# All projections in pairs of chunks, and attention's twelve steps in eight visits, in a two-layer encoder on one core

## The chip, the core and the metric

The kernel runs on one core of a Trainium2 chip. The core has five engines that run side by side, each through its own queue in order: TensorE (PE: matmuls and transposes, results in PSUM), VectorE (DVE), ScalarE (ACT), GpSimd (POOL), and SyncE (SP), which here issues nearly all DMA transfers. PE's loads of its stationary operand are listed apart, as PEld. PSUM has eight banks; this program uses four for projections and four for everything else. The metric is device time in microseconds of one execution; a kernel's time is the median of its runs.

## The reference

Two layers over 256 tokens of width 1024 in float32, each with a token mixer and a gated feed-forward part with a width-3 convolution. The change lies in the token mixer:

```python
u, q, k, v, g_pool, g_attn = jnp.split(xn @ w_in, SPLITS, axis=-1)
...
pooled = jnp.stack([_centred_mean(ug[:, :, gi], w) for gi, w in enumerate(POOL_WINDOWS)], axis=2) - ug
pool_out = jnp.einsum('bsgc,gcd->bsgd', pooled, w_pool).reshape(B, S, POOL_WIDTH) * pool_scale
...
outs.append(o_g)
lses.append(lse_g)
wts = jax.nn.softmax(jnp.stack(lses, axis=0), axis=0)
attn = jnp.einsum('gbsh,gbshd->bshd', wts, jnp.stack(outs, axis=0).astype(jnp.float32))
...
merged = jax.nn.sigmoid(g_pool) * (pool_out @ w_a) + jax.nn.sigmoid(g_attn) * (attn_out @ w_b)
return merged @ w_o
```

There are 12 heads of width 128 in three groups with dilations 1, 4 and 16. Head hh of each of the three groups is combined into output head hh, so four output heads remain.

## The kernel before, in words

**Precision by parts.** Every operand is split in two reduced-precision parts, high and low, and a product is the sum of high x high, low x high and high x low. The class `Weights` (line 95) loads 1 MB blocks of weights into three raw buffers by SP (L131) and splits each into pieces of 128 x 1024: ScalarE casts the high part `wh` (L191), VectorE subtracts for the low part `wl` (L192). Five pieces of each part are in SBUF at most (`BUFS`), and `get` splits up to three pieces past the one that it hands out. `free` gives a piece's buffers back.

**A chunk.** `proj` (L539) makes one chunk of 128 output columns for all 256 tokens. The moving operand holds the high and low parts of the activations side by side, so a chunk is eight wide matmuls (`wh`, 512 columns) and eight narrow ones (`wl`, 256 columns) into one PSUM bank, 16 in all. `proj(x2, n)` makes n chunks at one call of `two_sums` (L506), keeps the results in the list `ready`, and hands out one at a time; a later call takes what is ready and issues nothing. `two_sums` does all wide matmuls of its chunks and then all narrow ones, or the other way round, and turns the order round at each call, so that one call ends with the kind that the next begins with. The banks of a chunk are emptied by ScalarE and VectorE, by `add_up` (L567 and L568) for u, the gates and po2, and by L1055 to L1067 for q and k. Four banks (`mmp`) rotate among the projections, the pool sums and some smaller uses; four others (`acc`) serve values, attention and the output products.

**The order of a layer's token mixer.** Values; then u, eight chunks (L889 to L899), with the pooling windows on VectorE after every second; then q and k in six rounds m of four chunks (L1039), in the order `PAIRS`. In round m == 1 each of the four chunks comes after one of four pool parts (`pool_out`, L929), two calls of `two_sums` with two k-steps each, whose sums go through ScalarE (L943), VectorE (L944), ScalarE (L947) and VectorE (L948). From m == 3 on, one step of attention is issued after every second chunk. Then eight chunks over the pool outputs `po2` (L1074), with the other six steps between them; then eight chunks of gates, and so on.

**Attention's steps.** `scores(hh)` (L961): 14 matmuls into two banks, then VectorE (L976 adds the bias table `bt`, L981 takes the maximum), ScalarE (L984, the exponential) and VectorE (L986, L987). `turn(hh)` (L992): eight transposes of the probabilities (L999) into two banks, three copies by ScalarE and three operations of VectorE. `weigh(hh)` (L1010): 14 matmuls with the values, then one operation each of ScalarE and VectorE. Twelve steps are taken from a list, head a and head b of a pair interleaved:

```python
steps += [(scores, a), (turn, a), (scores, b), (weigh, a), (turn, b), (weigh, b)]
...
if m >= 3 and n % 2:
    step()
...
if c not in (1, 6):
    step()
```

Before, u was in single chunks in layer 0 and in pairs in layer 1 (`1 + (l > 0)`), q and k were in pairs but for m == 1, the chunks over po2 were single, and the gates were in pairs.

**What sets the order on an engine.** The framework orders instructions at build time by their place in the program and by when its timing model has their inputs ready; TensorE's order in the trace is that of the program in the changed stretch, while VectorE and ScalarE mix splits, emptying and attention as they come ready. `issue_after` ties a block behind a given instruction; it holds the bias table's transfers (L394 to L398), which are issued ahead of the first projection of pool group 1 in layer 0, behind the last weight load on SP.

Of the kernel before, what the change touches and what calls it, by code (L numbers as in the profile page):

```python
# [18 lines left out]
S = 256  # L19
# [12 lines left out]
PAD = 8  # L32
# [188 lines left out]
def encoder(ctx, tc, x, w_in, w_pool, pool_scale, w_a, w_b, w_o, norm1, norm2, w_up, conv_w,  # L221
# [13 lines left out]
    def cols(w, c0):  # L235

        src = w[:, c0 : c0 + 256].rearrange("(k p) c -> p k c", p=P)
        return W.add(
            src, (8, 256), [((lambda t, j=j: t[:, :, j * P : (j + 1) * P]), (8, P)) for j in (0, 1)]
        )  # L240
# [10 lines left out]
    for l in range(DEPTH):  # L251
# [24 lines left out]
        for c in range(2):  # L276
            W.use(cols(w_in[l], C_GA + c * 512))
            W.use(cols(w_in[l], C_GA + c * 512 + 256))
            src = w_b[l][:, c * 512 : (c + 1) * 512].rearrange("(k p) c -> p k c", p=P)
# [11 lines left out]
        for f in range(0, NF, 2):  # L291
            a = cols(w_up[l], f * P) if f >= ENTRY else []
# [213 lines left out]
    def two_sums(x2, nk, *chunks):  # L506

        wide, rests = ([(c, k, kind) for c in chunks for k in range(nk)] for kind in (True, False))
        first = rests if turns["rest"] else wide
        last = wide if turns["rest"] else rests
        for steps in (first, last):
            for (ps, wh, wl), k, kind in steps:
                out, w, x = (ps, wh, x2[:, k]) if kind else (ps[:, 1], wl, x2[:, k, 0])
                nc.tensor.matmul(  # L519
                    out, w(k), x, start=(steps is first and k == 0),  # L520
                    stop=(steps is last and k == nk - 1), skip_group_check=turns["rest"],
                )
        turns["rest"] = not turns["rest"]
# [15 lines left out]
    def proj(x2, n=1):  # L539


        if not ready:
            pieces = [W.get() for _ in range(n)]
            ps = [mmp.tile([P, 2, S], F32, tag="mm", name="proj_ps") for _ in range(n)]
            two_sums(
                x2, KD,
                *(
                    (b, lambda k, wh=wh: wh[:, k, :], lambda k, wl=wl: wl[:, k, :])
                    for b, (_, (wh, wl)) in zip(ps, pieces)
                ),  # L550
            )
            for i, _ in pieces:
                W.free(i)
            ready.extend((b[:, 0], b[:, 1]) for b in ps)
        return ready.pop(0)

    def halves(a):

        return a.rearrange("p (t m) -> p t m", t=2)

    def in_order(a):

        return a.rearrange("p (m t) -> p t m", t=2)

    def add_up(out, sums):

        nc.scalar.copy(out=out, in_=sums[1])  # L567
        nc.vector.tensor_add(out=out, in0=sums[0], in1=out)  # L568
# [90 lines left out]
    def two_parts(tag, name):  # L659


        return big.tile([P, KD, 2, 2, P], F32R, tag=tag, name=name)
# [174 lines left out]
    for l in range(DEPTH):  # L837
# [21 lines left out]
        if l == 0:  # L859
            with tc.manual_schedule():  # L860
                begun = begin_values_of_x()
            x2 = first_values(*begun, keep_values)
# [26 lines left out]
        for gi in range(3, -1, -1):  # L889
            w = WINDOWS[gi]  # L890
            u = sm.tile([P, 2, S + 2 * PAD], F32, tag="u", name="u")
            nc.vector.memset(u[:, :, 0:PAD], 0.0)
            nc.vector.memset(u[:, :, PAD + S :], 0.0)
            for j in range(2):
                if l == 0 and (gi, j) == (1, 0):

                    with tc.issue_after(W.last.ins):
                        next(bias)
                add_up(in_order(u[:, j, PAD : PAD + S]), [halves(a) for a in proj(x2, 1 + (l > 0))])  # L899
            cur, n = u, S + 2 * PAD  # L900
            sh = 1
            while sh < w:
                nxt = sm.tile([P, 2, S + 2 * PAD], F32, tag="us", name="us")
                n -= sh
                nc.vector.tensor_add(
                    out=nxt[:, :, 0:n], in0=cur[:, :, 0:n], in1=cur[:, :, sh : sh + n]
                )
                cur = nxt
                sh *= 2
            hw = w // 2  # L910
            o = PAD - hw
            e = edge[:, gi, 0:hw].unsqueeze(1).to_broadcast([P, 2, hw])
            nc.vector.tensor_mul(out=cur[:, :, o : o + hw], in0=cur[:, :, o : o + hw], in1=e)
            if hw > 1:
                e = edge[:, gi, hw : w - 1].unsqueeze(1).to_broadcast([P, 2, hw - 1])
                r = slice(o + S - hw + 1, o + S)
                nc.vector.tensor_mul(out=cur[:, :, r], in0=cur[:, :, r], in1=e)
            pd = sm.tile([P, 2, S], F32, tag="us", name="pd")
            nc.vector.scalar_tensor_tensor(
                out=pd, in0=cur[:, :, o : o + S], scalar=1.0 / w, in1=u[:, :, PAD : PAD + S],  # L920
                op0=ALU.mult, op1=ALU.subtract,
            )
            both = pl2[gi // 2][:, gi % 2 * 2 : gi % 2 * 2 + 2]
            ph, pl = both[:, :, 0], both[:, :, 1]
            pd = pd.rearrange("p k (m t) -> p k t m", t=2)
            nc.scalar.copy(out=ph, in_=pd)
            nc.vector.tensor_sub(out=pl, in0=pd, in1=ph.bitcast(F32))
            pooled[gi] = both
# [96 lines left out]
            nc.scalar.copy(out=oh, in_=ps)  # L1025
            nc.vector.tensor_sub(out=ol, in0=ps, in1=oh.bitcast(F32))

        steps = []
        for pair in ((0, 1), (2, 3)):
            a, b = pair  # L1030
            steps += [(scores, a), (turn, a), (scores, b), (weigh, a), (turn, b), (weigh, b)]

        def step():
            if steps:
                f, hh = steps.pop(0)
                f(hh)


        for m, c in enumerate(PAIRS):  # L1039
            if m == 1:  # L1040
                po2 = two_parts("m2", "po2")
                pool_parts = pool_out(po2)
            if m == 2:

                qkl = big.tile([P, 2, HPG, 2, P], F32R, tag="xn", name="qkl")
                ql, kl = qkl[:, 0], qkl[:, 1]
            for n in range(4):
                if m == 1:
                    next(pool_parts)
                src, rest = (halves(a) for a in proj(x2, 1 + (m != 1)))  # L1050
                hd = 2 * c + n % 2
                scale = HD**-0.5 if n < 2 else 1.0
                if hd < HPG:
                    hi, lo = ((qh, ql) if n < 2 else (kh, kl))
                    nc.scalar.mul(out=hi[:, hd], in_=src, mul=scale)  # L1055
                    nc.vector.scalar_tensor_tensor(
                        out=lo[:, hd], in0=src, scalar=scale, in1=hi[:, hd].bitcast(F32),
                        op0=ALU.mult, op1=ALU.subtract,
                    )
                    nc.vector.scalar_tensor_tensor(  # L1060
                        out=lo[:, hd], in0=rest, scalar=scale, in1=lo[:, hd].bitcast(F32),
                        op0=ALU.mult, op1=ALU.add,
                    )
                else:
                    o = (q if n < 2 else kk)[:, hd - HPG]
                    nc.scalar.mul(out=o, in_=rest, mul=scale)
                    nc.vector.scalar_tensor_tensor(  # L1067
                        out=o, in0=src, scalar=scale, in1=o, op0=ALU.mult, op1=ALU.add
                    )
                if m >= 3 and n % 2:  # L1070
                    step()

        pa = big.tile([P, KD, S], F32, tag="ybig", name="pa")
        for c in range(KD):  # L1074
            add_up(pa[:, c, :], proj(po2))
            if c not in (1, 6):
                step()
        assert not steps


        gates = big.tile([P, 4, S], F32, tag="gates", name="gates")
# [14 lines left out]
        for c4 in range(2):  # L1096
            ths = [gate(4 * c4 + j) for j in range(4)]
            for j2 in range(2):
# [3 lines left out]
                for j, ps in enumerate(both):  # L1102
                    c = 4 * c4 + 2 * j2 + j
                    m = sm.tile([P, S], F32, tag="u", name="m")
# [5 lines left out]
                    m = halves(m)  # L1110
# [4 lines left out]
        x2 = two_parts("x", "x2")  # L1115
# [114 lines left out]
        if l + 1 < DEPTH:  # L1230
            x2 = two_parts("x", "x2")
# [34 lines left out]
```

## Time and profile before

| | us |
|---|---|
| median of 3 runs | 875.19 |
| runs | 874.42 to 875.40 |
| the profiled execution | 874.7 |
| its span, first to last instruction | 872.8 |
| TensorE busy | 865.6 (99%) |
| VectorE busy | 680.1 (78%) |
| ScalarE busy | 526.1 (60%) |
| mean granted TensorE clock | 0.998 |

The page gives each engine's busy share in 40 slices of the span (digits are tenths), the chain of work that ended last, and groups of instructions with busy time, mean duration and the idle time before them. A row of the chain in order of time has a start, a length and what ran, with the number of matmuls behind x; its lengths run from one piece's modelled end to the next one's. A row of a timeline has start, length, engine, line, operation and operands. In both, L followed by a number is a line of the kernel.

### The profile page before, as it was taken

How to read it: one execution, taken by the hardware profiler on the slowest of the kernel's cores; microseconds unless marked ns; L12 is line 12 of the kernel's file. 1: busy time of each engine (PE TensorE's matmuls, PEld its weight loads, DVE VectorE, ACT ScalarE, POOL GpSimd, SP SyncE). 2: the span in 40 equal slices, each digit the busy share in tenths (PEclk: the TensorE clock that was granted, in tenths of full speed). 3: DMA queues.
4: the chain of work that ended last, by engine and by line, in shares of the span. 5: the costliest groups of instructions: out<-in, count | busy, mean ns of one | idle time of the engine just before them, and what ended most of it. 6: DMA issues, size and time to landing. Idle time of an engine off the chain costs nothing.

```text
span 872.8 us, 12725 instructions
## 1 busy us (share of the span) xinstructions
PE 865.6 (99%) x4807; PEld 756.8 (87%) x4807; DVE 680.1 (78%) x1158; ACT 526.1 (60%) x927; POOL 31.3 (4%) x98
## 2 busy tenths in 40 slices
PE   9999999999999999999999999999999999999997
PEld 8888889988888888888888889999888888888886
DVE  7998786757869978878855987776678698887874
ACT  7656554556647766666545674545666486666662
POOL 1800000000000000000000000000000000000000
PEclk9999999999999999999999999999999999999999
DMA  9676545345555475465636565453556446556531
GB/s 331 234 250 201 185 149 190 128 163 193 189 173 193 153 232 193 156 228 196 240 121 219 168 219 168 146 185 105 193 180 229 158 156 223 190 174 212 193 145 49
DMA packets 125958, 161.70 MB, mean 185 GB/s; under 512 B 3320, under 2 KB 106432, under 8 KB 125896
## 3 DMA queue, kind: packets, MB, share of 16 engines
q1 hardware_dynamic: 125736, 160.62, 54.7%
q8 instruction: 38, 0.62, 0.3%
q10 hardware_dynamic: 160, 0.27, 0.1%
q14 instruction: 24, 0.20, 0.1%
HBM read 159.80 MB, written 1.07 MB: 184 GB/s over the span
## 4 chain that ended last, share of the span: by engine, by line
PE 99%; DMA 0%; ACT 0%; POOLq 0%; issue 0%; DVE 0%; SPq 0%; POOL 0%; DVEq 0%; ACTq 0%
PE proj_ps L519 61%; PE v_ps L654 6%; PE res_ps L575 6%; PE res_ps L573 6%; PE res_ps L574 6%; PE b_ps L519 3%; PE v_ps L829 3%; PE v_ps L736 1%; PE pool_ps L519 1%; PE o_ps L1020 1%; PE s_ps L970 1%; PE pt_ps L999 1%; PE s_ps L965 1%; PE o_ps L1016 1%; PE xt_ps L457 1%; DMA raw<-in_w_in_dram 0%
## 5 line engine op out<-in xcount | busy, mean ns | idle before, releaser
L192 DVE TENSOR_TENSOR wl<-raw,wh 128x1024 fp32r<-128x1024 f32 x274 | 334.0, 1223 | 108.7 <-ACT wh L191 54.4
L191 ACT CAST wh<-raw 128x1024 fp32r<-128x1024 f32 x274 | 286.2, 1049 | 84.6 <-PE proj_ps L519 36.5
L519 PE MATMUL proj_ps<-x,wh 128*128 128x512 f32 x1408 | 335.0, 390 | 0.0
L519 PEld LDWEIGHTS proj_ps<-x,wh 128*128 128x128 f32 x1408 | 260.5, 188 | 51.7
L519 PEld LDWEIGHTS proj_ps<-x,wl 128*128 128x128 f32 x1408 | 176.7, 191 | 4.2
L519 PE MATMUL proj_ps<-x,wl 128*128 128x256 f32 x1408 | 179.8, 283 | 0.0
L573 PE MATMUL res_ps<-wh,actq 128*128 128x512 f32 (+1 forms) x184 | 70.0, 380 | 0.0
L574 PE MATMUL res_ps<-wl,actq 128*128 128x512 f32 (+1 forms) x184 | 69.9, 380 | 0.0
L575 PE MATMUL res_ps<-wh,actk 128*128 128x512 f32 (+1 forms) x184 | 69.9, 380 | 0.0
L574 PEld LDWEIGHTS res_ps<-wl,actq 128*128 128x128 f32 x184 | 34.6, 188 | 6.6
L575 PEld LDWEIGHTS res_ps<-wh,actk 128*128 128x128 f32 x184 | 34.6, 188 | 6.6
L573 PEld LDWEIGHTS res_ps<-wh,actq 128*128 128x128 f32 x184 | 34.6, 188 | 6.6
L1192 ACT ACTIVATE y<-y 128x256 f32<-128x256 f32 x44 | 18.1, 416 | 28.5 <-DVE y L1183 28.4
L519 PE MATMUL proj_ps<-po,wh 128*128 128x512 f32 x128 | 32.2, 396 | 0.0
L430 POOL TENSOR_SCALAR ss<-ss 128x1 f32<-128x1 f32 x8 | 2.0, 244 | 799.4 <-ACT junk L423 799.4
L1179 ACT ACTIVATE y<-a,prm 128x256 f32<-128x256 f32 x36 | 21.6, 600 | 14.8 <-DVE a L568 14.8
L519 PEld LDWEIGHTS proj_ps<-po,wh 128*128 128x128 f32 x128 | 23.1, 189 | 4.2
L573 PE MATMUL res_ps<-wh,m 128*128 128x512 f32 (+1 forms) x72 | 26.5, 368 | 0.0
L575 PE MATMUL res_ps<-wh,m 128*128 128x512 f32 (+1 forms) x72 | 26.3, 365 | 0.0
L574 PE MATMUL res_ps<-wl,m 128*128 128x512 f32 (+1 forms) x72 | 26.3, 365 | 0.0
L567 ACT COPY gates<-proj_ps 128x256 f32<-128x256 f32 x32 | 11.9, 373 | 23.4 <-PE proj_ps L519 23.4
L423 ACT ACTIVATE junk<-h 128x512 f32<-128x512 f32 (+1 forms) x19 | 10.5, 553 | 25.5 <-DVE h L421 25.3
(209 smaller groups left out, 1130.1 us busy)
## 6 DMA issues: line engine op xcount, KB each, us to landing
raw<-in_w_in_dram SPq DMA_DIRECT2D x58, 1024.0 KB, 5.2
raw<-in_w_up_dram SPq DMA_DIRECT2D x44, 1024.0 KB, 6.4
raw<-in_w_down_dram SPq DMA_DIRECT2D x22, 1024.0 KB, 4.9
raw<-in_w_a_dram SPq DMA_DIRECT2D x8, 1024.0 KB, 5.1
raw<-in_w_o_dram SPq DMA_DIRECT2D x8, 1024.0 KB, 4.8
raw<-in_w_b_dram SPq DMA_DIRECT2D x4, 1024.0 KB, 4.8
raw<-in_w_pool_dram SPq DMA_DIRECT2D x2, 1024.0 KB, 5.0
gain<-in_norm_dram SPq DMA_DIRECT2D x3, 512.0 KB, 4.3
```

The costliest lines, as they stand in the source:

```text
L191: lambda: nc.scalar.copy(out=h, in_=src),
L192: lambda: nc.vector.tensor_sub(out=l, in0=src, in1=h.bitcast(F32)),
L423: nc.scalar.activation(junk[:, 0 : cc.stop - cc.start], h[:, t, cc], AF.Square, scale=D**-0.5, accum_out=ss[:, n : n + 1],)
L519: nc.tensor.matmul(out, w(k), x, start=(steps is first and k == 0), stop=(steps is last and k == nk - 1), skip_group_check=turns["rest"],)
L567: nc.scalar.copy(out=out, in_=sums[1])
L573: nc.tensor.matmul(ps, ah, wh, start=first, stop=False, skip_group_check=on)
L574: nc.tensor.matmul(ps, ah, wl, start=False, stop=False, skip_group_check=on)
L575: nc.tensor.matmul(ps, al, wh, start=False, stop=last, skip_group_check=on)
L654: nc.tensor.matmul(ps, x2[:, 2 * n + j, part, t, :], w[:, j, :], start=(n + m == 0), stop=(n == 3 and m == 5),)
L829: nc.tensor.matmul(ps[t], a[:, k, t, :], w[:, j, :], start=(k + m == 0), stop=(k == KD - 1 and m == 2),)
L1179: nc.scalar.activation(y, a, AF.Identity, bias=b, scale=w1)
L1192: nc.scalar.activation(y2, y, AF.Square, scale=float(np.sqrt(0.044715)))
```

## The change

u in layer 0, q and k in m == 1, and the chunks over po2 are now made two at a call, as the others were, so that no single-chunk call is left in this part of the kernel. In m == 1 the pool parts stay where they were in the program; since the second chunk of a pair is ready when it is asked for, TensorE now gets part, pair, part, part, pair, part. Attention's twelve steps are the same, in nearly the same order, but are issued in eight visits: per pair of heads scores of a; turn of a with scores of b; weighing of a with turn of b; weighing of b. Four visits come after the pairs of rounds m == 3 and m == 4, none in m == 5, and four after the pairs over po2.

```diff
-                add_up(in_order(u[:, j, PAD : PAD + S]), [halves(a) for a in proj(x2, 1 + (l > 0))])
+                add_up(in_order(u[:, j, PAD : PAD + S]), [halves(a) for a in proj(x2, 2)])
...
-        steps = []
-        for pair in ((0, 1), (2, 3)):
-            a, b = pair
-            steps += [(scores, a), (turn, a), (scores, b), (weigh, a), (turn, b), (weigh, b)]
-
-        def step():
-            if steps:
-                f, hh = steps.pop(0)
+        visits = []
+        for a, b in ((0, 1), (2, 3)):
+            visits += [
+                [(scores, a)], [(turn, a), (scores, b)], [(weigh, a), (turn, b)], [(weigh, b)]
+            ]
+
+        def visit():
+            for f, hh in visits.pop(0):
                 f(hh)
...
-                src, rest = (halves(a) for a in proj(x2, 1 + (m != 1)))
+                src, rest = (halves(a) for a in proj(x2, 2))
...
-                if m >= 3 and n % 2:
-                    step()
+                if m in (3, 4) and n % 2:
+                    visit()
...
-            add_up(pa[:, c, :], proj(po2))
-            if c not in (1, 6):
-                step()
-        assert not steps
+            add_up(pa[:, c, :], proj(po2, 2))
+            if c % 2:
+                visit()
+        assert not visits
```

## The prediction

> **What bounds the kernel now.** I read the page first: the slices, then the chain that ended last; then the chain in order of time over the changed stretches, the timeline of VectorE around the attention steps, and the busy time by windows.
>
> ```profile
> span 872.8 us, 12725 instructions
> PE   9999999999999999999999999999999999999997
> DVE  7998786757869978878855987776678698887874
> PE 99%; DMA 0%; ACT 0%; POOLq 0%; issue 0%; DVE 0%; SPq 0%; POOL 0%; DVEq 0%; ACTq 0%
> L519 PE MATMUL proj_ps<-x,wh 128*128 128x512 f32 x1408 | 335.0, 390 | 0.0
> ```
>
> TensorE is the bound in every slice, and its 1408 wide projection matmuls have 0.0 us of idle time before them. The chain is 99% TensorE. So the time can fall only by what TensorE itself no longer spends, and it rises by every wait that reaches TensorE. VectorE is full in slices 1, 2, 12, 13 and 22 and has no share of the chain: it is cover that is nearly used up.
>
> The chain in order of time (start, length, what) gives the price of each piece:
>
> ```profile
> 40.94 33.38 PE proj_ps L519 x192
> ...
> 75.71 2.78 PE proj_ps L519 x16
> 78.49 1.41 PE pool_ps L519 x8
> 79.89 2.79 PE proj_ps L519 x16
> ...
> 109.31 5.57 PE proj_ps L519 x32
> 114.88 0.87 PE pt_ps L999 x8
> 115.75 5.59 PE proj_ps L519 x32
> ...
> 158.94 2.80 PE proj_ps L519 x16
> 161.74 0.71 PE o_ps L1016 x6
> 162.45 0.89 PE o_ps L1020 x8
> 163.34 2.81 PE proj_ps L519 x16
> ...
> 174.22 33.38 PE proj_ps L519 x192
> ...
> 471.06 33.34 PE proj_ps L519 x192
> ```
>
> x16 is one chunk alone, x32 a pair or two chunks. A chunk alone takes 2.78 to 2.81 us, a pair 5.55 to 5.60. The gates, twelve chunks in pairs, take 33.38 us, 2.782 each. The last row and the first are the same twelve chunks (u and the first two pairs of q and k) in both layers: layer 1, where u is already in pairs, 33.34 us; layer 0, with eight single chunks, 33.38.
>
> **The change, part by part.** No matmul is added or removed; each matmul, cast, subtraction and load stays.
>
> *Pairs for single chunks.* Layer 0 loses 4 calls of the two sums in u, 2 in m == 1, 4 over po2; layer 1 loses 2 and 4: 16 calls. The only row with and without is u: four calls fewer, 33.34 against 33.38, 0.04 us, so 0.01 us a call and 0.16 us for 16. The other rows agree in size: the single chunks of po2 cost 2.80, 2.79, 2.80, 2.81 against 2.78, so at most 0.03 a chunk.
>
> *Eight visits for twelve steps.* A layer loses four places at which TensorE goes from an attention step back to projections. Rows: the stretch behind a turn is 5.59 or 5.56, behind a weighing 5.55, behind scores 5.57, against 2 x 2.782 = 5.56. A place costs 0 to 0.03 us; four in two layers 0 to 0.24. I take 0.04 in all, since the rows lie nearer to nothing.
>
> *The ceiling.* In layer 0 the whole stretch from u to the gates is 174.22 - 40.94 = 133.28 us. Made of 40 chunks at 2.782 (111.28), four pool parts (1.40 + 1.41 + 1.39 + 1.41 = 5.61) and the steps (four scores at 1.61, four turns at 0.87, four weighings at 1.60: 16.32) it would be 133.21. So 0.07 us is there to be had in layer 0, and nearly nothing in layer 1 (604.27 - 471.06 = 133.21). The two ways give 0.07 and 0.20; I take **0.2 us**, with 0 and 0.4 as ends.
>
> *What must stay hidden.* (a) A pair takes two split weights before it gives one back, so of five buffers three, not four, run ahead; the loads on SP's queue keep their order, and the bias table's transfers, placed ahead of the first projection of pool group 1, are issued at the same place in it. Cover: u in layer 1 has this already, with VectorE at 5.43 of 5.50, 5.66 of 5.70 and 5.60 of 5.60 us in the windows from 476.5 to 493.3, and TensorE lost nothing. The table is read first at 109.32; its transfers are issued by 57.5, over 50 us earlier. So nothing; if the cover were gone, a cast and a subtraction (1.05 + 1.22 us) would show at a pair.
>
> (b) The turn waits for the softmax behind the scores:
>
> ```profile
> 109.32 1.28 DVE L976 TENSOR_TENSOR s<-s_ps,bt 128x512 f32<-128x512 f32 x2
> 110.52 1.27 DVE L981 TENSOR_REDUCE nm<-s 128x1 f32<-128x512 f32 x2
> 111.70 1.22 DVE L192 TENSOR_TENSOR wl<-raw,wh 128x1024 fp32r<-128x1024 f32 x1
> ...
> 113.03 0.88 DVE L987 TENSOR_SCALAR p<-p,rz 128x512 f32<-128x512 f32 x2
> ```
>
> The scores end at 109.31, the probabilities at 113.91: 4.6 us, and the turn comes 5.57 us after the scores, so 0.97 us are over. Heads 0 and 2 keep that distance of a pair. Heads 1 and 3 are new: their scores stand behind a turn in the same visit, whose three VectorE instructions (0.41 us each, L1004 and L1005) queue ahead of them, and their own turn comes after a pair and a weighing, 5.57 + 1.60 = 7.17 us. The longest chain in the trace (head 3, 158.94 to 164.50, two splits among it) is 5.56 us; with 1.24 it is 6.80. It still fits, by 0.4 us. The weighing waits for the turn's copies: done 3.1 us after the turn at 115.75 (118.82), and it now has 1.61 + 5.57 us. Nothing. What is queued behind a late turn is every projection after it, on TensorE.
>
> (c) PSUM in m == 1. Projections and pool sums share four banks. Before, a pool part (two banks) and a single chunk alternate. After, the order is part, pair, part, part, pair, part. Call the end of the q pair T. Its first chunk's sums end eight narrow matmuls earlier (some 0.95 us), the second's at T. The third part needs these banks at T + 1.40 and T + 2.10, the k pair the second part's at T + 2.81 and T + 3.76, whose sums ended at T + 0.70 and T + 1.40. So each bank has 2.1 to 2.4 us from its last sum to its next use. What emptying takes now, on VectorE:
>
> ```profile
> 88.98 0.42 DVE L1067 SCALAR_TENSOR_TENSOR k<-proj_ps,k 128x256 f32<-128x256 f32 x1
> 89.32 1.22 DVE L192 TENSOR_TENSOR wl<-raw,wh 128x1024 fp32r<-128x1024 f32 x1
> 90.45 0.87 DVE L944 SCALAR_TENSOR_TENSOR po<-pool_ps,hps,po 128x256 f32<-128x256 f32 x2
> ```
>
> The k chunk ended at 86.86 and was out at 89.40, 2.5 us; the pool part of 86.86 to 88.26 had its two sums out some 90.9 and 91.3, 3.3 and 3.1 us after; the quickest, the k1 chunk of 91.04, was out at 92.16, 1.1 us. None of these was urgent then: a weight split of 1.22 us was let in ahead. Bounds: no wait (1.1 us is well inside 2.1) and 3.3 - 2.1 = 1.2 us in each layer. VectorE is busy 11.94 of the 14.60 us from 73.5 to 88.1, 82%, and the q pair leaves 5.57 us without pool work in which splits can be got out of the way, so I take nothing and keep 2.4 us for both layers as the upper end. Here the Trainium skill speaks against the change. Its page "Perfetto Trace Analysis", section "Matmuls", says that independent groups should rotate through different banks so that emptying one overlaps the next group's matmuls; with two parts in a row and pairs around them the rotation comes round in 2.1 us, shorter than the rows' 2.5 to 3.3, and by that rule the second rival below comes true. The trace of before has no two parts in a row, so it shows neither.
>
> *Sum.* The profiled execution took 874.7 us (span 872.8 and 1.9 around it); less 0.2 is 874.5. It lies 0.5 under the median of the runs, 875.19, so for a median I say **875.0 us**. A difference under 0.2%, 1.75 us, is about what a measurement cannot tell from none.
>
> **The rivals.**
> 1. Forecast: everything new stays hidden; 874.8 to 875.2, with the runs' own spread 874.4 to 875.4. Chance 0.60.
> 2. PSUM banks come round too soon in m == 1 (c): waits of 0.2 to 1.2 us a layer, so 875.4 to 877.4, the middle 876.4. For: the rows above, 2.5 to 3.3 against 2.1. Against: splits can move into the pair. Chance 0.24, a quarter of it above 876.9.
> 3. On the slower side: the turn of heads 1 and 3 comes before its probabilities. It decides where one more split (1.22 us) gets in ahead of the softmax: 6.80 + 1.22 = 8.02 against 7.17, 0.85 us, four times, 3.4 us: 878.4. For: scores and a turn's copies now fall into one window, and VectorE was at 6.79 of 7.00 us with scores alone (107.7 to 114.7). Against: the 5.56 us chain holds two splits already. Chance 0.09.
> 4. The first pairs of u in layer 0 wait for a split (a): 2.3 us, 877.3. Against: layer 1. Chance 0.03.
> 5. Faster by more: the schedule of the other engines shifts and TensorE gains what no row shows. The ceiling of 0.07 us a layer speaks against; 1.75 us would be needed. Chance 0.04.
>
> Chances: faster by over 0.2% 0.04; slower by over 0.2% is rival 3 (0.09), a quarter of rival 2 (0.06) and rival 4 (0.03), 0.18; the same 0.78. The range takes in rivals 2 and 4 and the lower spread: 874.1 to 877.5.
>
> **What would show it.** Right: the chain is still 99% TensorE; u and the first two pairs in layer 0 take 33.34 us, the po2 pairs 5.56; the stretch from u to the gates is 133.1 to 133.2 us in both layers. Rival 2 shows as TensorE idle before pool_ps or the k pair in m == 1, released by VectorE (L944, L1067); rival 3 as idle before pt_ps at L999, released by L987; rival 4 as idle before proj_ps between 40 and 75 us. The forecast is wrong if TensorE idles anywhere in these for over 1 us, or if the stretch shrinks by more than 0.4 us without any.

## The result, and the profile after

The changed kernel takes 875.84 us in the median of 17 runs (875.29 to 878.0), the kernel before 874.55 (17 runs, 874.25 to 876.48): a ratio of 1.0016, 95% interval 1.0009 to 1.0024, so 1.3 us slower. The profiled execution took 875.4 us, its span 873.5. The forecast was 875.0 and "the same". The size of the change is under 0.2%, but its sign is the opposite of the forecast's -0.2 us.

The same rows of the page as those of before:

```profile
span 873.5 us, 12704 instructions
PE   9999999999999999999999999999999999999997
DVE  7998786757869978878855987676678699887874
PE 98%; DVE 1%; ACT 0%; issue 0%; POOLq 0%; POOL 0%; DVEq 0%; ACTq 0%
L519 PE MATMUL proj_ps<-x,wh 128*128 128x512 f32 x1408 | 334.6, 390 | 0.0
```

VectorE now has 1% of the chain, where it had none. The slices hardly differ, and the idle time before the group of wide projection matmuls is still 0.0. The chain in order of time tells where that 1% is, in layer 0:

```profile
40.57 33.34 PE proj_ps L519 x192
...
75.31 5.54 PE proj_ps L519 x32
80.84 2.80 PE pool_ps L519 x16
83.65 5.72 PE proj_ps L519 x32
...
114.60 0.87 PE pt_ps L999 x8
...
117.08 4.64 PE proj_ps L519 x24
121.81 0.85 DVE wl L192
122.66 0.29 issue
123.11 1.12 DVE wl L192
124.23 0.40 DVE p L987
124.78 0.63 PE pt_ps L999 x4
125.41 0.48 PE proj_ps L519 x4
125.89 0.44 PE pt_ps L999 x4
...
165.28 0.89 PE o_ps L1020 x8
166.18 1.07 PE pt_ps L999 x8
...
174.42 33.38 PE proj_ps L519 x192
```

u and the first two pairs take 33.34 us, as was said. Three places differ from the forecast. The k pair of round m == 1 takes 5.72 instead of 5.56 us. The turn of head 1 (124.78) is reached through VectorE: two weight splits (L192) and the last step of the softmax (L987). The turn of head 3 takes 1.07 instead of 0.87 us. From u to the gates layer 0 takes 174.42 - 40.57 = 133.85 us, 0.57 more than before; layer 1 has the same turns and takes 133.76, 0.55 more. The two add up to 1.12 us, most of the 1.3 us between the medians.

The turn of head 1 in the timeline, VectorE, ScalarE and TensorE together:

```profile
118.46 1.28 DVE L976 TENSOR_TENSOR s<-s_ps,bt 128x512 f32<-128x512 f32 x2
119.65 1.27 DVE L981 TENSOR_REDUCE nm<-s 128x1 f32<-128x512 f32 x2
120.83 1.05 ACT L191 CAST wh<-raw 128x1024 fp32r<-128x1024 f32 x1 [0.77 <-PE proj_ps L519]
121.78 0.72 ACT L984 ACTIVATE p<-s,nm 128x512 f32<-128x512 f32 x1
121.81 1.23 DVE L192 TENSOR_TENSOR wl<-raw,wh 128x1024 fp32r<-128x1024 f32 x1 [0.89 <-PE proj_ps L519]
...
123.03 1.21 DVE L192 TENSOR_TENSOR wl<-raw,wh 128x1024 fp32r<-128x1024 f32 x1
...
124.02 0.60 PE L519 MATMUL proj_ps<-x,wl 128*128 128x256 f32 x3
124.15 0.48 DVE L987 TENSOR_SCALAR p<-p,rz 128x512 f32<-128x512 f32 x1
...
124.78 0.63 PE L999 MATMUL pt_ps<-ident,p 128*128 128x128 f32 x4 [0.17 <-DVE rz L986]
124.94 0.48 DVE L987 TENSOR_SCALAR p<-p,rz 128x512 f32<-128x512 f32 x1
```

The number in brackets is the time that the engine stood idle before the instruction, and what ended it. The maxima are ready at 120.9, and yet ScalarE's exponential starts at 121.78: a weight cast stands ahead of it in the queue, and that cast itself stood 0.77 us until TensorE gave its buffer back. VectorE waits 0.89 us in the same way at a split, then puts a second split ahead of L987. The scores ended at 117.08 and the probabilities are done at 125.42: 8.34 us, not 6.80. TensorE had three narrow matmuls left to do first (124.02; at 0.12 us each and 0.08 for the return from attention they end at 124.46, by estimate) and stood still for 0.32 us; the transposes come in two halves with four more matmuls between. These narrow matmuls belong to the pair that follows the visit in the program, so here TensorE's order is not that of the program.

Head 3 is late in another way. No split on VectorE waits for a buffer there; two splits simply stand between the last steps of the softmax's two halves:

```profile
163.05 0.49 DVE L987 TENSOR_SCALAR p<-p,rz 128x512 f32<-128x512 f32 x1
163.66 1.22 DVE L192 TENSOR_TENSOR wl<-raw,wh 128x1024 fp32r<-128x1024 f32 x1
...
164.87 1.20 DVE L192 TENSOR_TENSOR wl<-raw,wh 128x1024 fp32r<-128x1024 f32 x1
165.99 0.48 DVE L987 TENSOR_SCALAR p<-p,rz 128x512 f32<-128x512 f32 x1
```

Its scores ended at 158.99 and its probabilities are done at 166.47: 7.48 us, where the turn comes after 7.19. The copies take more here than their own time. In the trace of before, VectorE began the first addition of the bias table ahead of the end of head 3's scores (158.94):

```profile
158.18 0.69 DVE L976 TENSOR_TENSOR s<-s_ps,bt 128x512 f32<-128x512 f32 x1
```

In the changed kernel both additions come behind the copies, from 160.04 on.

### The profile page after: what moved, and what is told of

Same layout as the page of the kernel before. It is cut to its first block, busy times and chain, and to the rows that moved or that the text cites. A ratio compares the mean times of both kernels' runs of the same rounds, so it can differ in the third digit from the quotient of the medians.

```text
span 873.5 us, 12704 instructions
## 1 busy us (share of the span) xinstructions
PE 866.1 (99%) x4807; PEld 756.2 (87%) x4807; DVE 678.8 (78%) x1158; ACT 527.7 (60%) x927; POOL 30.7 (4%) x98
## 3 DMA queue, kind: packets, MB, share of 16 engines
HBM read 159.80 MB, written 1.07 MB: 184 GB/s over the span
## 4 chain that ended last, share of the span: by engine, by line
PE 98%; DVE 1%; ACT 0%; issue 0%; POOLq 0%; POOL 0%; DVEq 0%; ACTq 0%
PE proj_ps L519 61%; PE v_ps L654 6%; PE res_ps L574 6%; PE res_ps L575 6%; PE res_ps L573 6%; PE b_ps L519 3%; PE v_ps L829 3%; PE v_ps L736 1%; PE pool_ps L519 1%; PE pt_ps L999 1%; PE s_ps L970 1%; PE s_ps L965 1%; PE o_ps L1020 1%; PE xt_ps L457 1%; PE o_ps L1016 0%; DVE wl L192 0%
## 5 line engine op out<-in xcount | busy, mean ns | idle before, releaser
L192 DVE TENSOR_TENSOR wl<-raw,wh 128x1024 fp32r<-128x1024 f32 x274 | 333.6, 1221 | 105.9 <-PE proj_ps L519 49.3
```

The costliest lines, as they stand in the source:

```text
L192: lambda: nc.vector.tensor_sub(out=l, in0=src, in1=h.bitcast(F32)),
```

## The experiments

Two theories of the turn were put against each other. **Splits:** weight splits, which may wait for their buffers, stand ahead of the softmax in ScalarE's and VectorE's queues. **Copies:** the turn's own three VectorE operations, now ahead of the next head's softmax, push it back. For round m == 1 there were **banks** (rival 2 of the prediction) and **load**: a weight load that comes late in layer 0. "Stretch" is the time from the first matmul of u to the first of the gates, by their starts; the chain's rows give 0.08 us more. A ratio stands against runs of the kernel before on the same chip.

| kernel | stretch, layer 0 | layer 1 | median | ratio, interval |
|---|---|---|---|---|
| before | 133.20 | 133.12 | 874.55 | |
| changed | 133.77 | 133.68 | 875.84 | 1.0016 (1.0009 to 1.0024) |
| splits behind the softmax | 133.96 | 133.14 | 874.61 | 0.9998 (0.9989 to 1.0007) |
| scores first | 133.26 | 133.06 | 874.42 | 1.0002 (0.9993 to 1.0011) |
| m == 1 single | 134.26 | 133.64 | 875.69 | 1.0016 (1.0007 to 1.0025) |
| old steps over q and k | 133.41 | 133.30 | 875.01 | 1.0007 (0.9998 to 1.0016) |
| before, u in pairs | 133.24 | 133.12 | 874.98 | 1.0003 (0.9994 to 1.0011) |
| before, m == 1 in pairs | 133.23 | 133.15 | 874.59 | 0.9997 (0.9988 to 1.0007) |
| scores first, u single | 133.10 | 133.06 | 874.46 | 0.9997 (0.9989 to 1.0006) |
| scores first, table in m == 2 | 133.05 | 133.06 | 874.05 | 0.9996 (0.9987 to 1.0005) |
| changed, table in m == 2 | 133.66 | 133.68 | 875.67 | 1.0017 (1.0008 to 1.0026) |
| splits behind, copies twice | 133.12 | 133.14 | 874.16 (one run) | |

### Splits behind the softmax

```diff
+                exp = nc.scalar.activation(p, s, AF.Exp, bias=nm[:, 0:1], accum_out=z)
...
+                norm_p = nc.vector.tensor_scalar(
...
+            if hh % 2:
+                W.queue_behind((exp, norm_p), 4)
```

> The changed kernel, with the next four weight splits after the scores of heads 1 and 3 tied behind the softmax on ScalarE and VectorE; the turn's three copies stay ahead of the softmax. Splits theory (the turn of heads 1 and 3 comes too early because splits that wait for their buffers stand ahead of the softmax in both queues): TensorE's idle before the transposes (0.32 us for head 1, 0.20 for head 3, in each layer) goes, the stretch from u to the gates falls from 133.85 to some 133.3 us in layer 0, the time by 1.0 us to about 874.8. Copies theory (it is the 1.24 us of the turn's own copies that push the softmax back): at least half of the idle stays, and the time falls by no more than 0.5 us.

The turn's copies stay where they are, and the wait is gone. Head 1 in the timeline:

```profile
117.12 0.41 DVE L1007 TENSOR_TENSOR ptl<-pt_ps,pth 128x256 fp32r<-128x256 f32 x1
...
118.65 1.27 DVE L981 TENSOR_REDUCE nm<-s 128x1 f32<-128x512 f32 x2
119.42 0.72 ACT L984 ACTIVATE p<-s,nm 128x512 f32<-128x512 f32 x1 [2.81 <-DVE nm L981]
...
120.84 1.99 ACT L191 CAST wh<-raw 128x1024 fp32r<-128x1024 f32 x2
...
121.17 0.49 DVE L987 TENSOR_SCALAR p<-p,rz 128x512 f32<-128x512 f32 x1
...
121.91 2.36 DVE L192 TENSOR_TENSOR wl<-raw,wh 128x1024 fp32r<-128x1024 f32 x2 [0.25 <-ACT wh L191]
...
124.69 1.04 PE L1001 MATMUL pt_ps<-ident,p 128*128 128x128 f32 x8
```

The exponential now starts as soon as the first maximum is there, the casts and splits come after it, and the probabilities are done at 121.66, 4.0 us after the scores instead of 8.3, with the same copies (here L1007) ahead. The transposes stand whole, 3 us after the probabilities. The median is 1.2 us under that of the changed kernel. Layer 1, 133.14, is back where it was before the change. Layer 0 did not fall (133.3 had been expected): this execution lost 0.8 us in round m == 1, which is the load theory's matter, below.

### Splits behind the softmax, and the copies twice

```diff
                     nc.vector.tensor_copy(pt[:, :, t, :], ps[:, 2:4, :])
+                    nc.vector.tensor_copy(pt[:, :, t, :], ps[:, 2:4, :])
...
+                nc.vector.tensor_sub(
+                    out=ptl[:, :, t, :], in0=ps[:, 0:2, :], in1=pth[:, :, t, :].bitcast(F32)
+                )
```

> The kernel with the splits tied behind the softmax of heads 1 and 3, with the bias table's reads in round m == 2, and with each of the turn's three VectorE operations done twice, most of the second ones ahead of the next head's softmax. Copies theory: 1.24 us more in front of the softmax brings TensorE's idle before the transposes of heads 1 and 3 back, 0.3 us or more each. Splits theory: the probabilities of heads 1 and 3 come some 1.2 us later than in the queued kernel (3.2 us before the turn there) and still in time, so no idle, 133.1 us in both layers.

The stretch is 133.12 and 133.14 us, with no idle before any turn. The probabilities of head 1 come at 121.79, 5.0 us after the scores (116.80), 1.0 later than in the kernel above and still in time. With the splits out of the way, twice the copies cost nothing, so the copies alone do not make the turn late. That does not make them free in the changed kernel, where copies and splits add up: without the copies' 1.24 us head 1 would be at 8.34 - 1.24 = 7.10 us, just inside the 7.17 (an estimate; no run takes the copies away). This kernel ran once.

### Scores of b ahead of the turn of a

```diff
-                [(scores, a)], [(turn, a), (scores, b)], [(weigh, a), (turn, b)], [(weigh, b)]
+                [(scores, a)], [(scores, b), (turn, a)], [(weigh, a), (turn, b)], [(weigh, b)]
```

> The changed kernel, with the scores of b ahead of the turn of a in their visit, so the softmax begins 0.87 us earlier and stands ahead of the turn's copies. Copies theory: the idle before the transposes of heads 1 and 3 goes and the time falls by about 1.0 us, to 874.8. Splits theory: it falls as far as the splits are now behind the softmax in the queues; one split of 1.22 us still stands ahead for head 1, and 0.87 us are gained, so most of the idle goes as well (874.8 to 875.2). Against both: if the weighing now waits for the turn's late copies, the idle moves to L1016.

874.42 us, no idle at the turns nor at the weighings; layer 1 at 133.06, 0.06 under the kernel before. Two splits still stand ahead of the end of head 1's softmax, and its probabilities come 7.1 us after its scores; but the turn now comes 8.0 us after them, some 0.87 us later than in the changed kernel. So this order mends the turns by giving the softmax more time, and it does not tell the two theories apart.

### The old steps over q and k

```diff
+        visits = [[(scores, 0)], [(turn, 0)], [(scores, 1)], [(weigh, 0)], [(turn, 1)], [(weigh, 1)]]
+        for a, b in ((2, 3),):
...
-                if m in (3, 4) and n % 2:
+                if m >= 3 and n % 2:
```

> The changed kernel, with the six steps of heads 0 and 1 one at a time over rounds 3 to 5 as before; heads 2 and 3 keep their visits over po2. Both theories of the turn: the idle of head 1 goes in both layers, that of head 3 stays (0.2 us a layer): the time falls by 0.6 to 0.7 us, to about 875.2. If the visits are not the cause: no change from 875.84.

875.01 us and 133.30 in layer 1, 0.38 less than the changed kernel: head 1's idle is gone and head 3's 0.2 us stay, as expected. So the cost is paid at each of the two heads whose scores share a visit with a turn; what is left in layer 1, 0.18 us over the kernel before, is head 3's.

### Round m == 1

> The changed kernel, with the chunks of round m == 1 single again. Banks theory (PSUM banks come round too soon in m == 1): the 0.13 us before the k pair in layer 0 and the 0.04 in layer 1 go, less 0.04 us for four calls: the time falls by 0.1 us, which no verdict can tell, and the trace shows no idle between 74 and 92 us. If round m == 1 costs more in undisturbed executions than the one profile shows, the time falls by up to 1 us.

```diff
-                src, rest = (halves(a) for a in proj(x2, 2))
+                src, rest = (halves(a) for a in proj(x2, 1 + (m != 1)))
```

875.69 us: no change that can be told. But the idle in m == 1 was expected to go, and in this execution layer 0 lost more there than in the changed kernel's profile, with single chunks:

```profile
75.43 3.07 PE proj_ps L519 x16
...
84.14 3.03 PE proj_ps L519 x16
```

Two of these chunks take 3.07 and 3.03 us instead of 2.78, and layer 1 shows nothing of the kind. So it is not the pairs of this round. The opposite edit to the kernel before agrees:

> The kernel before with round m == 1 in pairs, nothing else changed. Banks theory (four PSUM banks come round in 2.1 us, sooner than they are emptied): TensorE idles 0.1 to 0.4 us before the k pair in both layers, the time rises by 0.2 to 0.8 us. Load theory: with u single there is no late load, and the idle is 0 to 0.1 us in layer 0 as it was 0.04 in layer 1; the time stays at 874.4 within 0.2.

133.23 and 133.15 us, 0.03 more than before in each layer, no idle above 0.02 us, 874.59: the banks theory fails. What else is only in layer 0 is the bias table. SyncE's queue in the changed kernel:

```profile
52.52 0.37 SPq L131 DMA_DIRECT2D raw<-in_w_pool_dram  x1
52.99 5.01 SPq L398 DMA_DIRECT2D bt<-fd  x5
59.50 16.97 SPq L131 DMA_DIRECT2D raw<-in_w_in_dram  x4
```

The next weight load is issued at 59.50, behind five reads of the table. In pairs the cast that needs it is reached at 64.2, and ScalarE, all its queue behind that cast, stands still until the load has landed:

```profile
66.77 1.05 ACT L191 CAST wh<-raw 128x1024 fp32r<-128x1024 f32 x1 [2.61 <-DMA raw<-in_w_in_dram]
```

In the kernel before, with u single, ScalarE's waits for such loads come to 0.7 us in the window from 55 to 92 us. Counted from the first matmul of u, pairs make the load 0.7 us later (19.09 against 18.37 us) and reach its cast 0.9 us earlier (23.75 against 24.63).

> The kernel before with u of layer 0 in pairs, nothing else changed. Load theory (a pair asks for its weights earlier, one load stands behind the bias table's transfers on SP, ScalarE's queue stands behind the cast that waits for it, and PSUM is emptied late in m == 1): ScalarE waits some 3 us for a weight load near 64 us, TensorE idles 0.1 to 0.7 us between 74 and 92 us, and the time rises by 0.1 to 0.6 us, to 874.5 to 875.1. Against: u and the first two pairs take 33.34 us and nothing else changes, 874.4.

Here, with u in pairs alone, the cast waited 2.4 us and TensorE lost 0.08 us at one chunk of m == 1 (2.86 instead of 2.78), less than the 0.1 that was expected at least. The median, 874.98, lies in the expected range, but a ratio of 1.0003 (0.9994 to 1.0011) does not show a rise. The profiles side by side tell more. The table gives the longest wait of that cast, and the stretch of layer 0 over that of layer 1, which is 0.08 in the kernel before:

| kernel | wait of the cast | layer 0 over layer 1 |
|---|---|---|
| before, u in pairs | 2.4 | 0.12 |
| old steps over q and k | 2.5 | 0.11 |
| changed | 2.6 | 0.09 |
| scores first | 2.7 | 0.20 |
| m == 1 single | 2.9 | 0.62 |
| splits behind the softmax | 3.1 | 0.82 |

In these six profiles a wait of up to 2.6 us goes with some 0.1 us of TensorE's time, one of 2.9 or 3.1 us with 0.6 or 0.8. The time from the load's issue to the cast differs as much, from 7.1 to 7.8 us, so the cost differs from one execution to the next.

> The changed kernel with the scores of b ahead of the turn of a, and u of layer 0 single again. Load theory: the idle in m == 1 of layer 0 goes; the stretch from u to the gates is 133.1 us in both layers and the time some 874.2, 0.2 under the scores-first kernel with u in pairs. Banks theory: the idle before the k pair stays in both layers and the time stays at 874.4.

With u single the wait is down to 0.6 us and layer 0 takes 133.10 us, as expected; the median, 874.46, does not show so little.

> The changed kernel with the scores of b ahead of the turn of a, u in pairs, and the five reads of the bias table moved from u to round m == 2, behind the weight load that was issued last there. Load theory: the weight loads of u come on time, the idle in m == 1 of layer 0 goes, the stretch in layer 0 falls to 133.1 us and the time to 874.1 to 874.3. Otherwise: no change from 874.4; if the table now hinders the loads of m == 2, the idle moves there.

```diff
         nc.sync.dma_start(out=fd[0].rearrange("(h e) -> h e", h=HPG), in_=fsb)
+        yield
...
             if m == 2:
+                if l == 0:
+                    with tc.issue_after(W.last.ins):
+                        next(bias)
```

With u in pairs and the table's reads at 82.84 us instead of 52.99, no cast waits for a load in the window, and the chain has nothing but plain pieces:

```profile
41.77 33.34 PE proj_ps L520 x192
...
76.51 5.55 PE proj_ps L520 x32
82.06 2.81 PE pool_ps L520 x16
84.86 5.59 PE proj_ps L520 x32
...
125.32 0.87 PE pt_ps L1000 x8
```

The late load itself is not issued any earlier for it. SyncE's queue in this kernel:

```profile
53.73 0.37 SPq L131 DMA_DIRECT2D raw<-in_w_pool_dram  x1
60.72 22.08 SPq L131 DMA_DIRECT2D raw<-in_w_in_dram  x5
```

It comes 6.99 us after the pool weights' load here and 6.98 in the changed kernel. What differs is the transfer: here the load has landed 4.85 us after its issue, while with the table's reads ahead of it the cast started 7.1 to 7.8 us after it (the six kernels of the table above). In the 3.5 us before the issue the core's transfers run at 324 GB/s in the changed kernel, and at 106 GB/s in the changed kernel with the table in m == 2. So the load is late because the table's transfers are still under way, not because their issue holds up its own.

The two layers take 133.05 and 133.06 us, 0.21 us less than the kernel before in sum. This is the best version: 874.05 us, a ratio of 0.9996 (0.9987 to 1.0005), which the timing cannot tell from the kernel before; the stretches in the two traces differ by 0.21 us.

> The changed kernel with only the five reads of the bias table moved from u to round m == 2. Splits and load theory as two separate causes: layer 0 now costs what layer 1 costs, 133.68 us from u to the gates, with the idle before the transposes of heads 1 and 3 (0.32 and 0.20 us) and none above 0.05 us in m == 1; the time lies 0.1 to 0.4 us under the changed kernel's 875.84, at about 875.5. If the idle at the turns comes from the late load as well, it goes in layer 0.

133.66 and 133.68 us: layer 0 now costs what layer 1 costs, the turns of heads 1 and 3 keep their 0.32 and 0.20 us in both, and the median is 875.67. The two causes are separate, and the turns are nearly all of the loss: 0.1 us of the changed kernel's 133.77 in layer 0 is the load's.

## Why the prediction was wrong

- **What bounds the kernel** was right: TensorE, from end to end, so that any wait that reaches it is paid in full.
- **The gain of 0.2 us** came out only in part. u in layer 0 fell from 33.38 to 33.34 as said. But round m == 1 in pairs alone cost 0.03 us a layer where 0.02 of gain was forecast, and with both waits taken away in the forecast's own order of visits (splits behind, copies twice, table in m == 2) the two stretches fall by 0.08 us and rise by 0.02, 0.06 less in all. The 0.21 us, by 0.15 and 0.06, came with the scores of b ahead of the turn of a. That this agrees with the 0.2 is luck in part; where the difference between the two orders lies is open.
- **Step (b) failed, and decided the sign.** It said that the softmax of heads 1 and 3 takes 5.56 us and 1.24 for the copies, 6.80 against 7.17, "still fits, by 0.4 us". It took 8.34 for head 1 and 7.48 for head 3. The copies' term was not the one that was off: with twice the copies, and the splits out of the way, the softmax took 5.0 us. The term that was too small is the chain of 5.56 us. At head 1 it took the splits as work of 1.22 us each; but a split at the head of a queue can itself wait for a buffer that the running pair holds (0.77 us on ScalarE, 0.89 on VectorE), and all behind it waits with it, the softmax on both engines. At head 3 the splits were plain work on VectorE, two of them as assumed; but the 5.56 us had a head start, the first addition of the bias table, which was under way before the scores ended and now comes behind the copies. With the splits tied behind the softmax the idle went at both heads: it is the splits ahead of it, on top of the copies, that make the turn late.
- **Rival 3** named the place, the sign in the trace and the kind of mechanism (splits ahead of the softmax), with a chance of 0.09; but it reckoned with one more split of 1.22 us, and the trace has two on VectorE, as the chain of before had. Its price, 0.85 us four times, was too high: the turns cost 0.32 and 0.20 us, twice each. At head 1 the probabilities came 1.17 us too late (8.34 against 7.17), and seven narrow matmuls of the next pair, ahead of the turn and between its halves, filled most of it; at head 3 they came 0.3 us too late.
- **Step (a)** was right for layer 1 and wrong for layer 0. "Layer 1 has this already" left out the one thing that layer 1 lacks, the table's transfers; a load that was issued after them landed late and made ScalarE wait 2.4 to 3.1 us. Rival 4 had the place but not the mechanism. In the profile of the changed kernel it costs 0.1 us; in others of the executions up to 0.8.
- **Step (c)** was right to take no wait: m == 1 in pairs alone costs 0.03 us a layer. The page "Perfetto Trace Analysis" of the Trainium skill, section "Matmuls", asks that groups rotate through different banks so that emptying overlaps; the four banks still allowed that here (133.23 and 133.15 us). The 0.16 us at the k pair that looked like this rival in the changed kernel were gone with the bias table's reads moved.
- **What stays open:** how a late cast near 64 us turns into idle time of TensorE only between 75 and 85 us was not followed step by step; that it does is shown by the idle time that goes when the table is moved.

## What to carry to other kernels

When one engine is busy from end to end, a chain of other engines that feeds it must be counted with the whole in-order queue ahead of it, and each entry there with the wait that it may itself bring, not with its duration alone. Work with a near deadline (here a softmax) belongs ahead of work that runs far in advance (the weight splits): tying the one behind the other gave the 1.2 us back. And an argument that another part of the program does the same already holds only when the transfers under way are the same too.

## What was not expected of the hardware

The time from the first instruction to the first matmul of u, with the same work in all these kernels, was 40.23 to 42.11 us over the profiled executions (40.77 before, 42.11 with m == 1 in pairs), while the 296.9 us between the two stretches and the 268.8 after the second agree within 0.2 us in all of them. So the opening alone moves a run by up to 1.9 us, more than the change that was to be measured, and a stretch of one's own in the trace tells 0.1 us where the whole time tells 0.8. The kernel of 42.11 us was profiled in a run of 875.97 us, 1.4 above its median. Single runs lie further off, up to 2.2 us above the median for the changed kernel and for the kernel before alike, and 3.1 us for one of the changed kernel with the table in m == 2; no profile fell on such a run, so whether the opening is the cause there is not shown.
